# One-core streaming encoder layer: the out-projection's product halves one behind the other, its first token tile begun inside the last value product

## The chip, the cores and the metric

The kernel runs on one core of a Trainium2 chip. The metric is the device time of one execution in microseconds (us). Five engines run side by side, each working through its own instructions in a fixed order: PE multiplies matrices (PEld is its weight load), ACT and DVE do elementwise work, POOL does small elementwise work, SP issues the DMAs. The order on every engine is written when the kernel is built, by a planner that plays the program through with estimated durations and picks, for each engine, the ready instruction of the highest priority (roughly, the one written first). On the chip an instruction waits for semaphores but is never overtaken on its engine.

## What is computed

One inference step of a one-layer encoder, for 1024 prompt tokens and 32 tokens of a running stream (1056 in all), width 1024:

```
h  = mixer(rms_norm(x, g_mix_pre))          # proj = xn @ w_in, three kinds of recurrent heads
                                            # cat = heads' outputs, normed and gated
                                            # mixer returns cat @ w_out   <- the out-projection
x  = x + rms_norm(h, g_mix_post)
h  = conv_ffn(rms_norm(x, g_ffn_pre))       # up @ w_up, causal conv, gelu(gate)*val, @ w_down
x  = x + rms_norm(h, g_ffn_post)
```

All matrices are float32. A product is made of three passes of a faster format: an operand is split into a high part and a low part (high by a cast on ACT, low by a subtraction on DVE or POOL), and `mm3` adds high*high, high*low and low*high in PSUM. In the profile these are lines 100, 101 and 102.

## The kernel before

The tokens are nine tiles `u`: 0 to 7 of 128 prompt tokens, 8 of the 32 running tokens. Three groups `g` (tiles 0-2, 3-5, 6-8) pass through the input projection one after the other. In each, `inproj` makes the feature products, then the value and gate columns in blocks of 256 (`blk` 0 to 7; 0-3 values, 4-7 gates). For the last group `vg_across` makes them with the tokens across: for each of two halves `e` 24 matmuls (8 `k` times 3) into one PSUM bank `pv`, an ACT copy to an SBUF tile `vf` (line 460), and then, behind the next block's products, `back`: per token tile two PE transposes into a bank `pb` (line 448) and `vg_store`, which for the gates is tanh on ACT (line 420, recorded as line 112), one or two steps on DVE, a multiply on POOL (line 427) and a store to DRAM. `vf` is taken in the pool `p1` under the tag `x`.

The heads' recurrences, `mixer(u)`, are a side stream: a generator advanced a few steps after each step of the main stream (`merge`, `pump`). Its small matmuls (line 702) and DVE, ACT and POOL steps stand between the main stream's work on all engines. While the out-projection runs, the mixers of tiles 8, 6 and 7 are still going, in this order, each behind the one before; the out-projection's tiles come in the order `RING` = 0, 1, 2, 3, 8, 4, 5, and then 6 and 7.

The out-projection of a tile, `outproj(u)`, in parts divided by `yield`:

- load `cat` of the tile (`ct`, line 268) and the residual `xr` (line 275), and those of the next tile;
- for each half of the columns four transposes of `ct` into a bank `ctp` (line 1031), the split into `ch` (ACT, line 1035) and `cl` (DVE, line 1036), in the pool `p2`, three buffers each;
- the product `zp`: for each `k` of 8 the three matmuls of the first 512 columns and the three of the second, so that two PSUM banks fill side by side; for tile 0 `out_weights` splits the weight row `k` in front of it (`woh` by ACT, lines 106 and 1001; `wol` by DVE, lines 109 and 1003; from the raw rows `wor`);
- for each bank a square with its sum and a copy to `z` on ACT (lines 1066, 1067);
- the norm and the residual (POOL lines 1069, 218, 219; DVE lines 1076, 1077; ACT line 1081), and the transposes `fxt` of the result (PE line 1100, two banks; DVE line 1105), stored to DRAM for the FFN.

`pipeline` runs them so that a tile's transposes come before the last part of the tile two back, then the norm of the tile one back, then the tile's product. PSUM has one pool, `psb`, of three banks (tag `big`) for `pv`, `pb`, `ctp`, `zp` and `fxt`; the mixers have others, one of them the bank `mi` in two halves, handed out in turn by `small`.

SBUF is used again by pools that open and close: `p2`, with the 8-row tiles `woh` and `wol`, is opened where `p1` was closed. The FFN's first pools stand where the mixers' pools were.

Of the kernel before, what the change touches and what calls it, by code (L numbers as in the profile page):

```python
# [8 lines left out]
F32 = mybir.dt.float32  # L9
# [10 lines left out]
DEC = 32  # L20
# [70 lines left out]
def body(ctx: ExitStack, tc: tile.TileContext, a: dict):  # L91
# [163 lines left out]
    pws, wo_raw, ring = ExitStack(), [], []  # L255
    NRING, CT0 = 7, 6

    ct_of, xr_of, tail, xlate, mixed = {}, {}, [], {}, set()
# [11 lines left out]
    def load_res(u):  # L270
        if u in xr_of:
            return
        n = 128 if u < 8 else DEC
        xr_of[u] = (ring if u in RING else tail)[0](f"xr{u}")
        sp.dma_start(xr_of[u][:n], xsrc(128 * u, n))

    def units_of(g):
        t0, pl, sl = GROUPS[g]
        us = [(t0 // 128 + i, 128 * i, 128) for i in range(pl // 128)]
        if sl:  # L280
            us.append((8, pl, sl))
        return us
# [71 lines left out]
    def inproj(g, xh, xl, normed, scaled=None):  # L354
# [87 lines left out]
        def vg_across(blks):  # L442

            def back(blk, fs, part):
                for (u, off, n) in units_of(g)[part]:
                    ps = psb.tile([128, 256], F32, tag="big", name=f"pb{u}_{blk}")
                    for e in range(2):
                        pe.transpose(ps[:n, 128 * e:128 * e + 128], fs[e][:, off:off + n], ident)
                    vg_store(blk, u, off, n, ps)

            before = None
            for blk in blks:
                ws = vg_weights(blk)
                fs = p1.tile([128, 2, T], F32, tag="x", name=f"vf{blk}", bufs=3)
                fs = [fs[:, 0], fs[:, 1]]
                for e in range(2):
                    ps = psb.tile([128, T], F32, tag="big", name=f"pv{g}_{blk}_{e}")
                    for k in range(8):
                        mm3(ps, [w[:, 128 * e:128 * e + 128] for w in ws[k]], (xh[:, k, :], xl[:, k, :]), k == 0, k == 7)
                    act.copy(fs[e], ps)  # L460
# [207 lines left out]
        if g == 2:  # L668
            pfs.close()
            pw = pws.enter_context(tc.tile_pool(name="pw", bufs=1, side="left"))  # L670
            ring.append(lambda name: pw.tile([128, 1024], F32, tag="ring", name=name, bufs=NRING))
            for k in range(8):
                if k == CT0:
                    load_cat(0)
                wo_raw.append(ring[0](f"wor{k}"))
                sp.dma_start(wo_raw[k], a["w_out"][k])
# [327 lines left out]
            yield  # L1004


    def outproj(p2, W, u):

        gm, woh, wol = W[:3]
# [9 lines left out]
        ct = ct_of[u]  # L1019
        chs = []  # L1020
        for hf in range(2):
            if u < 7 or u == 8:
                ps = psb.tile([128, 4, 128], F32, tag="big", name=f"ctp{u}{hf}")
            else:
# [4 lines left out]
            for k in range(4):  # L1029
                c = 512 * hf + 128 * k  # L1030
                pe.transpose(ps[:, k, :n], ct[:n, c:c + 128], ident[:n, :n])
            ch = p2.tile([128, 4, 128], F32R, tag="ch", name=f"ch{u}{hf}", bufs=3)
            cl = p2.tile([128, 4, 128], F32R, tag="cl", name=f"cl{u}{hf}", bufs=3)
            with tc.high_priority(offset=AHEAD):
                ins = (act.copy(ch[:, :, :n], ps[:, :, :n]),
                       dve.tensor_tensor(cl[:, :, :n], ps[:, :, :n], ch[:, :, :n].bitcast(F32), op=ALU.subtract))
            if u == RING[0]:
                halves[:] = ins
            chs += [(ch[:, k, :n], cl[:, k, :n]) for k in range(4)]
        yield  # L1040
        ss = p2.tile([128, 4], F32, tag="oss", name=f"oss{u}", bufs=2)
        pss = [psb.tile([128, 512], F32, tag="big", name=f"zp{u}{hf}") if u != 7 else
               upper[0].tile([128, 512], F32, tag="xw", name=f"zp{u}{hf}", bufs=4) for hf in range(2)]
        cs = [slice(512 * hf, 512 * hf + 512) for hf in range(2)]
        if u == 7:

            jk = jks[0]
            for hf in range(2):
                for k in range(8):
                    mm3(pss[hf], chs[k], (woh[:, k, cs[hf]], wol[:, k, cs[hf]]), k == 0, k == 7)  # L1050
                with tc.high_priority(offset=AHEAD):
                    kept["jk"] = act.activation(jk, pss[hf], AF.Square, accum_out=ss[:, hf:hf + 1])
        else:
            for k in range(8):
                if u == RING[0]:
                    next(W[3])
                for hf in range(2):
                    mm3(pss[hf][:n], chs[k], (woh[:, k, cs[hf]], wol[:, k, cs[hf]]), k == 0, k == 7)
                if k == 3 and u == 6:
                    yield  # L1060
        load_res(u)
        x = xr_of[u]
        if u != 7:
            z = (ring if u in RING else tail)[0](f"z{u}")
            for hf in range(2):
                act.activation(z[:n, cs[hf]], pss[hf][:n], AF.Square, accum_out=ss[:n, hf:hf + 1])
                act.copy(z[:n, cs[hf]], pss[hf][:n])
# [44 lines left out]

    def pipeline(gens):

        for i in range(len(gens) + 2):
            for j in (i, i - 2, i - 1, i):
                if 0 <= j < len(gens) and i - 1 < len(gens):
                    next(gens[j])
                    yield


    def col_operands(pool_, q, s, between=lambda: None):
# [359 lines left out]
    pool.memset(x0[:, :, 1, smp:smp + 2], 0.0)  # L1482
    firsts = [outproj(p2, wo, u) for u in RING]
    merge(pipeline(firsts), 27, 3 * NMIX + 2)
    pump(1000)
    last = [outproj(p2, wo, u) for u in (6, 7)]
    for x in (last[0], last[0], last[1]):
        next(x)
    sp.dma_start(x0[:, :, 0, :], xn_d[:, :, 0:n0])
    sp.dma_start(x0[:, :, 1, :smp], xn_d[:, :, HW:HW + smp])  # L1490
    sp.dma_start(x0[:, :, 1, smp + 2:smp + 130], xn_d[:, :, fcol(4):fcol(5)])
# [210 lines left out]
```

## Time and profile before

| | |
|---|---|
| median of 3 runs | 1419.99 us (1419.96 to 1420.18) |
| the profiled execution: its time | 1421.18 us |
| the profiled execution: span from first to last instruction | 1419.4 us |
| PE busy | 1368.0 us (96%) |
| DVE busy | 1009.2 us (71%) |
| ACT busy | 711.3 us (50%) |
| POOL busy | 281.9 us (20%) |
| mean granted TensorE clock | 0.986 |

How to read the profile: times are microseconds from the span's start. A row of the timeline has start, duration, engine, line, operation, output and inputs, shapes and count; in brackets stands the idle time of the engine before it and what ended it. A row of the windows has the stretch, its length, then for PE, PEld, DVE, ACT and POOL the busy time and the number of instructions, then the TensorE clock that was granted (1.00 is full speed), the DMA share and GB/s. The matmuls' durations overlap their neighbours', so the pace of a row of matmuls is read from their starts.

### The profile page before, as it was taken

The page shows a single profiled execution, that of the slowest core. Times are in us where ns is not written, and L with a number is a line of the kernel's source. Part 1 is how long each engine was busy: PE and PEld are TensorE (multiplying, and loading weights), DVE is VectorE, ACT ScalarE, POOL GpSimd, SP SyncE. Part 2 cuts the span into 40 slices and gives each one's busy share as a digit, 9 for nine tenths or more (in the row PEclk, how much of TensorE's full clock was granted, in tenths as well). Part 3 has the DMA queues.
Part 4 walks back from the last instruction along what each step waited for, and adds up shares of the span by engine and source line. Part 5 has one row for each costly group of instructions (what it writes and reads, how often), then busy time and mean ns, then how long its engine had stood idle before and what let it go on. Part 6 is the DMA issues. An engine that isn't in the chain of part 4 may idle for free.

```text
span 1419.4 us, 30029 instructions
## 1 busy us (share of the span) xinstructions
PE 1368.0 (96%) x11804; PEld 1253.1 (88%) x11804; DVE 1009.2 (71%) x1818; ACT 711.3 (50%) x1403; POOL 281.9 (20%) x461
## 2 busy tenths in 40 slices
PE   6989999999999998899899999999999999999998
PEld 5989889998888876767799999999999999988886
DVE  4795469758687667676798887788888875654644
ACT  4555447445474545333755545554455544533432
POOL 5531211224112223212131111111111110000100
PEclk9999999999999989999999999999999999999999
DMA  9599779776789753344412221221222156765652
GB/s 344 191 338 342 242 238 309 232 254 210 270 281 341 256 179 125 129 145 102 138 50 99 79 91 70 91 76 73 79 82 85 62 199 239 235 221 169 245 176 100
DMA packets 132581, 255.11 MB, mean 180 GB/s; under 512 B 27639, under 2 KB 78487, under 8 KB 132439
## 3 DMA queue, kind: packets, MB, share of 16 engines
q1 hardware_dynamic: 132439, 253.19, 52.3%
q8 instruction: 92, 1.51, 0.4%
q14 instruction: 50, 0.41, 0.1%
HBM read 192.26 MB, written 60.89 MB: 178 GB/s over the span
## 4 chain that ended last, share of the span: by engine, by line
PE 78%; DVE 8%; DMA 5%; ACT 4%; issue 2%; POOL 2%; SPq 1%; DVEq 0%; POOLq 0%; ACTq 0%
PE pd L102 6%; PE pd L101 6%; PE pd L100 6%; PE pux L100 4%; PE pux L102 4%; PE pux L101 4%; PE pv L100 3%; PE pv L102 3%; PE pv L101 3%; PE puw L101 3%; PE puw L100 3%; PE puw L102 3%; PE zp L100 2%; PE pf L100 2%; PE pf L101 2%; PE zp L101 2%
## 5 line engine op out<-in xcount | busy, mean ns | idle before, releaser
L1276 DVE SCALAR_TENSOR_TENSOR y<-uu,fconv_sb,y 128x1060 f32<-128x1060 f32 x88 | 116.2, 1321 | 28.5 <-ACT y L1274 27.8
L102 PE MATMUL pd<-wd,hl 128*128 128x512 f32 x264 | 105.0, 399 | 0.0
L101 PE MATMUL pd<-wd,hh 128*128 128x512 f32 x264 | 104.1, 394 | 0.0
L100 PE MATMUL pd<-wd,hh 128*128 128x512 f32 x264 | 103.5, 393 | 0.0
L1270 POOL COPY uu<-uu 128x2 f32<-128x2 f32 x44 | 36.6, 831 | 214.2 <-DVE uu L1218 214.0
L1213 ACT COPY c<-pux 128x274 f32<-128x274 f32 (+1 forms) x132 | 49.3, 376 | 40.8 <-PE pux L102 39.5
L1274 ACT ACTIVATE y<-uu,fconv_sb 128x1060 f32<-128x1060 f32 x44 | 56.1, 1275 | 16.9 <-POOL uu L1271 15.6
L100 PE MATMUL zp<-woh,ch 128*128 128x512 f32 (+1 forms) x144 | 59.1, 414 | 5.3 <-DVE z L1105 5.2
L100 PE MATMUL pv<-wt_0h,xh 128*128 128x256 f32 (+2 forms) x195 | 58.6, 301 | 5.6 <-ACT xh L318 5.4
L101 PEld LDWEIGHTS pd<-wd,hh 128*128 128x128 f32 x264 | 49.6, 188 | 12.6
L100 PEld LDWEIGHTS pd<-wd,hh 128*128 128x128 f32 x264 | 49.6, 188 | 11.7
L102 PEld LDWEIGHTS pd<-wd,hl 128*128 128x128 f32 x264 | 49.6, 188 | 11.5
L101 PE MATMUL zp<-wol,ch 128*128 128x512 f32 (+1 forms) x144 | 58.4, 405 | 0.0
L102 PE MATMUL pv<-wt_0h,xl 128*128 128x256 f32 (+2 forms) x195 | 57.6, 296 | 0.4 <-DVE xl L319 0.4
L102 PE MATMUL zp<-woh,cl 128*128 128x512 f32 (+1 forms) x144 | 57.6, 403 | 0.0
L101 PE MATMUL pv<-wt_0l,xh 128*128 128x256 f32 (+2 forms) x195 | 57.2, 293 | 0.1
L100 PE MATMUL pv<-wt_1h,xh 128*128 128x256 f32 (+2 forms) x195 | 56.8, 291 | 0.0
L102 PE MATMUL pv<-wt_1h,xl 128*128 128x256 f32 (+2 forms) x195 | 56.7, 291 | 0.0
L101 PE MATMUL pv<-wt_1l,xh 128*128 128x256 f32 (+2 forms) x195 | 56.5, 290 | 0.0
L100 PE MATMUL pd<-hh,wd 128*128 128x288 f32 x176 | 52.0, 296 | 0.0
L101 PE MATMUL pd<-hl,wd 128*128 128x288 f32 x176 | 52.0, 296 | 0.0
L102 PE MATMUL pd<-hh,wd 128*128 128x288 f32 x176 | 51.8, 296 | 0.0
(1678 smaller groups left out, 5138.6 us busy)
## 6 DMA issues: line engine op xcount, KB each, us to landing
h_d<-y SPq DMA_DIRECT2D x22, 530.0 KB, 2.7
wt_0r<-in_w_tok SPq DMA_DIRECT2D x21, 512.0 KB, 6.1
wt_1r<-in_w_tok SPq DMA_DIRECT2D x21, 512.0 KB, 6.5
wt_0l<-lt_d SPq DMA_DIRECT2D x14, 512.0 KB, 7.1
wt_1l<-lt_d SPq DMA_DIRECT2D x14, 512.0 KB, 7.6
hr<-h_d SPq DMA_DIRECT2D x44, 128.0 KB, 3.1
hr<-h_d SPq DMA_DIRECT2D x22, 192.0 KB, 3.2
x<-in_xp SPq DMA_DIRECT2D x8, 512.0 KB, 7.6
```

Source lines behind the costliest of these rows:

```text
L100: pe.matmul(ps, lh[0], rh[0], start=first, stop=False, **kw)
L101: pe.matmul(ps, lh[0], rh[1], start=False, stop=False, **kw)
L102: return pe.matmul(ps, lh[1], rh[0], start=False, stop=last, **kw)
L1213: kept[name] = act.copy(t, ps)
L1270: pool.tensor_copy(u[:, GAP_P:GAP_P + 2], u[:, GAP_S - 2:GAP_S])
L1274: act.activation(y, u, AF.Identity, scale=fconv[:, j, 2:3], bias=fconv[:, j, 3:4])
L1276: dve.scalar_tensor_tensor(y, uu[i][:, s:s + NCOL], fconv[:, j, s:s + 1], y, op0=ALU.mult, op1=ALU.add)
```

## The change

It does four things. The tile `vf` gets a pool of its own, `pvf`, opened when group 2's feature pools close and closed after tile 0's product. In the last block of `vg_across` the transposes back of the block before all go behind `k` = 3 of the first half, and behind `k` = 3 of the second half stand the first four transposes and the split of the out-projection's tile 0 (`cat_half`, into `pvf`); the last block's own are written behind its second half, tiles 6 and 7 in one bank (`both`), and tile 8 of the last two blocks in a half of the bank `mi`. The product of every tile of `RING` but the first is made one half of the columns behind the other, each followed by its square and copy, and `pipeline` puts the next tile's transposes behind the halves: first half, the next tile's first four transposes, second half, the next tile's other four, the last part of the tile before, the norm of this one. The residual `xr` is loaded after the transposes, for the own tile alone, no longer one tile ahead; the FFN's first columns `xg0` are opened, and the two gap columns cleared, after tile 0's product.

```diff
@@ vg_across (inproj)
             def back(blk, fs, part):
+                late = blk >= blks[-1] - 1
+                both = psb.tile([128, 2, 256], F32, tag="big", name=f"pb67_{blk}") if blk == blks[-1] else None
                 for (u, off, n) in units_of(g)[part]:
-                    ps = psb.tile([128, 256], F32, tag="big", name=f"pb{u}_{blk}")
+                    ps = small(256) if late and u == 8 else both[:, u - 6] if both is not None else \
+                        psb.tile([128, 256], F32, tag="big", name=f"pb{u}_{blk}")
...
-                fs = p1.tile([128, 2, T], F32, tag="x", name=f"vf{blk}", bufs=3)
+                fs = vfs[0].tile([128, 2, T], F32, tag="vf", name=f"vf{blk}", bufs=3)
                 fs = [fs[:, 0], fs[:, 1]]
+                last = blk == blks[-1]
                 for e in range(2):
                     ps = psb.tile([128, T], F32, tag="big", name=f"pv{g}_{blk}_{e}")
                     for k in range(8):
                         mm3(ps, [w[:, 128 * e:128 * e + 128] for w in ws[k]], (xh[:, k, :], xl[:, k, :]), k == 0, k == 7)
+                        if last and k == 3:
+                            if not e:
+                                back(*before, slice(0, 3))
+                            else:
+                                first_half.append(cat_half(vfs[0], RING[0], 0))
                     act.copy(fs[e], ps)
-                    if before:
+                    if before and not last:
                         back(*before, slice(e, 1 + 2 * e))
                     yield
                 before = (blk, fs)
                 yield
-            for e in range(2):
-                back(*before, slice(e, 1 + 2 * e))
+            back(*before, slice(0, 3))
@@ inproj, g == 2, behind pfs.close() and the ring's pool
+            vfs.append(pvs.enter_context(tc.tile_pool(name="pvf", bufs=1, side="left")))
@@ outproj
+    def cat_half(p, u, hf, ps=None, **kw):
+        n = 128 if u < 8 else DEC
+        if ps is None:
+            ps = psb.tile([128, 4, 128], F32, tag="big", name=f"ctp{u}{hf}")
+        for k in range(4):
+            c = 512 * hf + 128 * k
+            pe.transpose(ps[:, k, :n], ct_of[u][:n, c:c + 128], ident[:n, :n])
+        ch = p.tile([128, 4, 128], F32R, tag="ch", name=f"ch{u}{hf}", **kw)
+        cl = p.tile([128, 4, 128], F32R, tag="cl", name=f"cl{u}{hf}", **kw)
...
+        return [(ch[:, k, :n], cl[:, k, :n]) for k in range(4)]
...
         load_cat(u)
         if u in RING:
-            load_res(u)
-            nxt = (RING + (6,))[RING.index(u) + 1]
-            load_cat(nxt)
-            if nxt in RING:
-                load_res(nxt)
+            load_cat((RING + (6,))[RING.index(u) + 1])
...
+            chs += first_half.pop() if u == RING[0] and not hf else cat_half(p2, u, hf, ps, bufs=3)
+            if u in RING:
+                yield
+        if u not in RING:
+            yield
+        if u in RING:
+            load_res(u)
...
+        def leave(ps, hf):
+            act.activation(z[:n, cs[hf]], ps[:n], AF.Square, accum_out=ss[:n, hf:hf + 1])
+            act.copy(z[:n, cs[hf]], ps[:n])
+
+        if u == RING[0]:
+            pss = [bank(hf) for hf in range(2)]
+            for k in range(8):
+                next(W[3])
+                for hf in range(2):
+                    product(pss[hf], hf, k)
+            z = ring[0](f"z{u}")
+            for hf in range(2):
+                leave(pss[hf], hf)
+            first_columns()
+            yield
+        elif u in RING:
+            z = ring[0](f"z{u}")
+            for hf in range(2):
+                ps = bank(hf)
+                for k in range(8):
+                    product(ps, hf, k)
+                leave(ps, hf)
+                if not hf:
+                    yield
...
     def pipeline(gens):
-        for i in range(len(gens) + 2):
-            for j in (i, i - 2, i - 1, i):
-                if 0 <= j < len(gens) and i - 1 < len(gens):
-                    next(gens[j])
-                    yield
+        next(gens[0])
+        next(gens[0])
+        yield
+        for i, x in enumerate(gens):
+            after = gens[i + 1:i + 2]
+            next(x)
+            yield
+            for y in after:
+                next(y)
+            yield
+            next(x)
+            yield
+            for y in after + gens[i - 1:i] + [x]:
+                next(y)
+            yield
...
-    x0 = p3s.enter_context(tc.tile_pool(name="p3", bufs=1, side="right")).tile([128, 8, 2, SUBS[0][1]], F32, name="xg0")
-    xlate[0] = x0
-    pool.memset(x0[:, :, 1, smp:smp + 2], 0.0)
+    def first_columns():
+        pvs.close()
+        xlate[0] = p3s.enter_context(tc.tile_pool(name="p3", bufs=1, side="right")).tile(
+            [128, 8, 2, SUBS[0][1]], F32, name="xg0")
+        pool.memset(xlate[0][:, :, 1, smp:smp + 2], 0.0)
...
-    merge(pipeline(firsts), 27, 3 * NMIX + 2)
+    merge(pipeline(firsts), 26, 3 * NMIX + 2)
```

Tiles 6 and 7 keep the order of their products as it was.

More of the change, by code (lines that the diff above doesn't have):

```diff
@@ L1028, in outproj @@
                 ps = both[:, hf]
[L1029 to L1036, printed above, removed]
@@ new lines, in outproj @@
+        if u == RING[0]:
+            pss = [bank(hf) for hf in range(2)]
[17 more added lines that the diff above has]
+                    yield
+        elif u == 6:
+            pss = [bank(hf) for hf in range(2)]
+            for k in range(8):
+                for hf in range(2):
+                    product(pss[hf], hf, k)
+                if k == 3:
+                    yield
+            z = tail[0](f"z{u}")
+            for hf in range(2):
+                leave(pss[hf], hf)
+        else:
+            pss = [bank(hf) for hf in range(2)]
@@ L1049, in outproj @@
                 for k in range(8):
-                    mm3(pss[hf], chs[k], (woh[:, k, cs[hf]], wol[:, k, cs[hf]]), k == 0, k == 7)
+                    product(pss[hf], hf, k)
                 with tc.high_priority(offset=AHEAD):
                     kept["jk"] = act.activation(jk, pss[hf], AF.Square, accum_out=ss[:, hf:hf + 1])
[L1053 to L1060, printed above, removed]
         load_res(u)
         x = xr_of[u]
[L1063 to L1067, printed above, removed]
         yield
```

27 lines of the change are left out of this document (15 added, 12 removed).

## The prediction

> **What bounds the kernel now.** I read the page first: busy times and the chain that ended last.
>
> ```profile
> PE 1368.0 (96%) x11804; PEld 1253.1 (88%) x11804; DVE 1009.2 (71%) x1818; ACT 711.3 (50%) x1403; POOL 281.9 (20%) x461
> PE 78%; DVE 8%; DMA 5%; ACT 4%; issue 2%; POOL 2%; SPq 1%; DVEq 0%; POOLq 0%; ACTq 0%
> ```
>
> PE is the bound of the whole, so a gain must be PE's idle time or PE's slow time. The change touches one stage, from the end of the last value product to the end of tile 7's product, so I asked for the windows of that stage, cut where the granted clock changes.
>
> ```profile
> core 0: us, PE busy (x) PEld busy (x) DVE busy (x) ACT busy (x) POOL busy (x), PEclk, DMA share, GB/s
> 511.10:515.40 4.30, 3.89 (x84) 2.71 (x83) 3.15 (x11) 1.10 (x4) 1.46 (x3) 0.99 0.09 30
> 515.40:529.00 13.60, 12.80 (x59) 9.05 (x58) 10.75 (x22) 9.71 (x13) 3.19 (x4) 0.50 0.90 301
> 529.00:538.70 9.70, 9.70 (x55) 7.59 (x54) 3.06 (x4) 1.66 (x5) 0.00 (x0) 1.00 0.64 202
> 538.70:604.00 65.30, 56.54 (x637) 45.29 (x637) 52.42 (x112) 30.71 (x77) 24.17 (x33) 1.00 0.37 121
> 604.00:607.50 3.50, 3.50 (x20) 2.08 (x15) 3.50 (x9) 0.72 (x2) 0.00 (x0) 0.51 0.00 0
> 607.50:664.00 56.50, 53.85 (x600) 39.88 (x597) 36.38 (x83) 19.13 (x45) 12.72 (x25) 1.00 0.39 118
> 664.00:689.30 25.30, 25.30 (x122) 20.86 (x122) 21.59 (x26) 16.43 (x33) 4.29 (x8) 1.00 0.59 187
> ```
>
> Two things are to be seen. From 515.4 to 529.0 PE ran at half clock: 12.80 us of work that would take 6.4 at full clock. And from 538.7 to 664 PE stood idle for 8.76 + 2.65 = 11.4 us. Third, PE's waits in that last stretch, to see what the idle time was for (waited for; total, times, longest), the largest of them:
>
> ```profile
> PE zp L100 <- DVE z L1105: 5.2, 3, 2.9
> PE om L702 <- DVE w L927: 2.3, 1, 2.3
> PE ctp L1031 <- ACT z L1067: 1.4, 1, 1.4
> PE fxt L1100 <- DVE z L1105: 0.6, 1, 0.6
> PE fxt L1100 <- ACT z L1067: 0.6, 1, 0.6
> ```
>
> Four of these are not waits for data. The product `zp`, the transposes `ctp` and `fxt` wait until ACT or DVE has read an older bank out: there are three banks, and the product holds two. They make 5.2 + 1.4 + 0.6 + 0.6 = 7.8 us. Only the 2.3 is a mixer's. Fourth, the timelines around tile 0:
>
> ```profile
> 510.76 0.30 PE L102 MATMUL pv<-xh,wt_1l 128*128 128x288 f32 x1
> 510.90 0.60 PE L448 MATMUL pb<-ident,vf 128*128 128x128 f32 x4
> 511.10 0.40 ACT L460 COPY vf<-pv 128x288 f32<-128x288 f32 x1 [2.73 <-PE pv L102]
> 515.36 1.99 ACT L106 CAST woh<-wor 128x1024 fp32r<-128x1024 f32 x2 [1.54 <-PE pb L448]
> 520.27 1.12 PE L1031 MATMUL ctp<-ident,ct 128*128 128x128 f32 x4 [0.61 <-ACT vth L112]
> 521.04 0.78 PE L100 MATMUL zp<-woh,ch 128*128 128x512 f32 x1
> 526.88 4.82 DVE L1003 TENSOR_TENSOR wol<-wor,woh 128x1024 fp32r<-128x1024 f32 x4
> 538.35 0.39 PE L102 MATMUL zp<-woh,cl 128*128 128x512 f32 x1
> ```
>
> The last value product ends at 511.06, but tile 0's begins at 521.04 and ends at 538.7. ACT's first weight cast waited for the transposes `pb`: `woh` lies where `p1` was, and `p1` held `vf`, which those transposes read last. And `ctp` waited 0.61 us for a bank that a tanh still had to read.
>
> **The change part by part.** First, the start of tile 0. With `vf` in its own pool the first cast waits for the last value product and ACT's copy behind it, so it starts at 511.5 instead of 515.36, 3.9 us earlier.
>
> ```profile
> L106 ACT CAST woh<-wor x2: 1040/1042/1044, 515.4 to 516.3; 128x1024 fp32r<-128x1024 f32 x2
> L109 DVE TENSOR_TENSOR wol<-wor,woh x2: 1218/1222/1225, 516.4 to 517.6; 128x1024 fp32r<-128x1024 f32 x2
> 549.08 0.39 PE L102 MATMUL zp<-woh,cl 128*128 128x512 f32 x1
> 551.80 0.39 PE L102 MATMUL zp<-woh,cl 128*128 128x512 f32 x1
> ```
>
> One cast and one subtraction later, at 511.5 + 1.04 + 1.22 = 513.8, the first product can run, since its `ch` and `cl` (first half) are ready by then. How early can tile 0 end? By DVE: its last weight subtraction ended at 531.70; 3.9 earlier is 527.8. The rows of 549.08 and 551.80 are twelve matmuls apart, 0.227 us each; six follow the last subtraction, so 529.2. By PE: 27.6 us from 511.1 to 538.7, less 1.2 idle, less 6.4 for the half clock, leaves 20.0 us of work, so 531.1: 7.6 us earlier if the clock doesn't fall. If it falls as before at 515.4, it should return as long after the first dense product as now (529.0 - 521.04 = 8.0), at 521.8. Then 6.4 us at half clock cost 3.2, the end is 534.3, and the gain 4.4. I take 5, near the second, because what stands before 515.4 stays transposes and small mixer matmuls. The moved transposes themselves cost nothing new: the block's own six and tile 0's eight were there before, four in 0.60 us or less; inside the value product they wait for nothing, since tile 0's `cat` is loaded long before.
>
> The banks `both` and `mi`: tiles 6 and 7 in one bank leave one for `ctp`, which takes the 0.61 (inside the 5). In exchange tile 7's transposes may wait for tile 6's tanh, and a mixer's matmul for tile 8's: 0 to 0.61 each, two blocks, at most 1.2. PE has value products or tile 0's to run beside it, so I take 0 and keep 1.2.
>
> Second, the products one half behind the other, six tiles.
>
> ```profile
> L1066 ACT ACTIVATE z<-zp x16: 581/598/651, 538.3 to 684.1; 128x512 f32<-128x512 f32 x14, 32x512 f32<-32x512 f32 x2
> L1067 ACT COPY z<-zp x16: 557/585/661, 539.9 to 687.2; 128x512 f32<-128x512 f32 x14, 32x512 f32<-32x512 f32 x2
> ```
>
> The matmuls are the same 48 a tile. A half is 24 x 0.227 = 5.4 us, and its bank is read out in 0.60 + 0.59 = 1.2. So the first half leaves under the second, and behind a product PE waits for one bank where it waited for two. I take half of the 7.8 away: 4. The ends are all of it, 7.8, and below nothing: another wait of 0.6 for each of five later tiles, 3 us lost. The ACT work is the same; where it stands in ACT's queue is the second rival.
>
> Third, the queues. On SP the load of `xr` comes one tile later.
>
> ```profile
> DMA to landing us min/median/max: 2.6/4.7/7.5
> 515.38 0.11 POOL L1482 MEMSET xg<- 128x16 f32 x1 [0.16 <-PE pb L448]
> ```
>
> It lands in 4.7 us, 7.5 at most, and its reader, DVE's add, comes behind the own product of 10.9 us: hidden; without that cover it would cost up to 7.5 per tile. The loads of `cat` keep their lead of one tile. POOL's 0.11 us for the gap columns move behind tile 0; the pool's first other user is the FFN. The 26 for 27 in `merge` moves the mixers' steps by a twenty-seventh. All this I count at nothing.
>
> What is late next: tile 7 and the FFN's beginning.
>
> ```profile
> 665.42 0.87 POOL L906 TENSOR_TENSOR cat<-cat,gt 128x320 f32<-128x320 f32 x1
> 666.32 0.33 SPq L1160 DMA_DIRECT2D wu0r<-in_w_up  x1
> 678.28 0.48 PE L100 MATMUL zp<-woh,ch 128*128 128x512 f32 x1
> ```
>
> Mixer 7 delivers the last part of its `cat` at 666.29, and tile 7's product begins at 678.28. Transposes (0.60), cast and subtraction (an estimate: half of the weights' 1.04 and 1.22, as half as wide) lie between, so 10 us are slack: a gain of 9 on PE fits even if the mixers stood still. But the FFN's first load leaves right behind mixer 7, so the mixers must move too.
>
> The sum: 5 + 4 = 9 us off the span of 1419.4, 1410.4. The profiled execution took 1421.18, 1.8 more than its span and 1.2 more than the median; so 1412.2 for a profiled one, and 1411.0 beside the median of 1419.99.
>
> **The rivals.** First, the mixers set the end. Mixers 8, 6 and 7 follow one another, and DVE is busy 52.42 of 65.3 us. If mixer 7 still ends at 666.3, the FFN starts as before, and only DVE's idle time from 664.0 to 689.3 can be gained, 25.3 - 21.59 = 3.7. I would expect 1.5 of it, 1418.5. Against it speaks who waits for whom between 510 and 680:
>
> ```profile
> DVE cl L1036 <- ACT ch L1035: 11.6, 5, 6.6
> DVE S L872 <- PE mi L702: 6.6, 4, 4.4
> DVE hn L965 <- PE om L702: 3.4, 1, 3.4
> ACT z L1066 <- PE zp L102: 41.3, 6, 13.9
> ```
>
> The mixers' DVE steps wait 6.6 + 3.4 for PE, PE only 2.3 for theirs. They are pushed back by the products and should move up with them.
>
> Second, slower: ACT held. ACT takes its queue in order; six times it stood at the head of a tile's square, 41.3 us in all, and in these six holds DVE waited 11.6 us for casts behind it, 1.9 a hold. With two squares per tile there are six holds more, now with mixers' exponentials behind them. At 1.9 each that is 11.6 us and takes the 4 away too: -5 + 11.6 = 6.6 slower, 1426.6. It decides from 1.5 us a hold (9 / 6). Against it: the first half's square waits while the second half's matmuls run, so PE has work.
>
> Third, the clock stays down as long. If the half clock lasts its 13.6 us wherever the products begin, of the first term only the 1.2 us of idle time are left, and 1.2 + 4 = 5.2 give 1414.8. For it: the long stretch held 12.80 us of instructions and still did not raise the clock until eight us of dense products; against it: those began late. [...]
>
> **How the numbers follow.** A measurement here can tell about 0.2%, 2.8 us, from no change. Forecast 0.50, mixers 0.17, ACT held 0.17, clock 0.16. The forecast and the clock rival lie beyond 2.8 us on the fast side (0.49 and 0.16), of the mixers' rival 0.05 does: faster 0.70. Its other 0.12 and 0.01 of the forecast are the same: 0.13. Slower 0.17. The forecast's own ends: 7.6 + 7.8 off, and 1.8 more if the half clock at 604 goes, 17.2, 1402.8; and 4.4 - 3 - 1.2 off, about nothing. The range from 1403 to 1422 holds these and the mixers' rival, and cuts off most of the held ACT (0.12) and a little at the fast end (0.04).
>
> **What would show it.** Right: the first `woh` cast at about 511.5 behind the copy `vf` and not behind `pb`; tile 0's last `zp` between 531 and 535; less than 8 us at half clock around it; the bank waits of `zp`, `ctp` and `fxt` at about 4 us in sum; mixer 7's last `cat` and the load `wu0r` about 9 us earlier; from there on the FFN's length unchanged. Wrong: `cat` of tile 7 still at 666 (first rival); ACT's waits for `zp` longer in sum and DVE or PE waiting behind ACT (second); 13 us at half clock (third). New waits of PE inside the last value product would break the first term.

## The result, and the profile after

The changed kernel takes 1428.04 us (median of six runs, 1426.94 to 1429.13); the kernel before, on the same chip and in the same set, 1421.59. The ratio is 1.0044, with a 95% interval from 1.003 to 1.0059: slower by 6 us. The forecast was 1411.0, faster. The profiled execution took 1426.94 us with a span of 1425.2, 5.8 more than before.

From the head of the kernel after's page, its span and the engines' busy times:

```profile
span 1425.2 us, 30044 instructions
...
PE 1368.0 (96%) x11804; PEld 1253.2 (88%) x11804; DVE 1008.2 (71%) x1818; ACT 711.1 (50%) x1403; POOL 279.0 (20%) x461
```

PE is busy for the same 1368.0 us as before. What was lost is idle time of PE: 57.2 us against 51.4. The windows of the stage, with the same bounds as in the prediction, show that it didn't come where the change begins:

```profile
511.10:515.40 4.30, 3.54 (x29) 2.33 (x26) 3.95 (x6) 4.30 (x6) 0.77 (x2) 1.00 0.79 240
515.40:529.00 13.60, 12.53 (x72) 9.65 (x72) 9.93 (x20) 8.39 (x17) 3.76 (x6) 1.00 0.61 194
529.00:538.70 9.70, 9.70 (x53) 7.77 (x52) 5.16 (x7) 4.44 (x11) 0.75 (x2) 1.00 0.81 292
538.70:604.00 65.30, 55.80 (x612) 42.74 (x610) 45.55 (x99) 25.23 (x61) 20.85 (x28) 0.90 0.36 117
604.00:607.50 3.50, 3.50 (x19) 1.93 (x18) 3.44 (x10) 1.62 (x4) 2.08 (x2) 1.00 0.43 108
607.50:664.00 56.50, 55.31 (x620) 43.05 (x620) 36.59 (x85) 17.85 (x43) 13.74 (x23) 0.91 0.33 106
```

The granted clock (the last column but two) is 1.00 up to 538.7: the half clock of 13.6 us before is gone. Behind 538.7 it is 0.90 and 0.91, where before it was 1.00 but for 3.5 us. Now the timeline of tile 0 and of its surroundings:

```profile
510.91 2.00 ACT L106 CAST woh<-wor 128x1024 fp32r<-128x1024 f32 x2
512.01 0.50 PE L100 MATMUL zp<-woh,ch 128*128 128x512 f32 x1
526.02 0.39 PE L102 MATMUL zp<-woh,cl 128*128 128x512 f32 x1
```

Tile 0's product starts 9.0 us earlier than before and ends at 526.4, 12.3 us earlier. PE's waits from 510 to 695 follow (total, times, longest):

```profile
PE ctp L1027 <- DMA ct<-cat_d: 4.6, 1, 4.6
PE zp L100 <- DVE cl L1032: 2.5, 1, 2.5
PE sc L713 <- DVE P L807: 2.3, 2, 1.9
...
PE fxt L1151 <- DVE cl L1032: 0.8, 1, 0.8
...
PE zp L100 <- ACT z L1074: 0.3, 1, 0.3
```

Of the 7.8 us of waits for banks, 3.6 are left: the 0.3, and also the 2.5 and the 0.8, since the matmuls of line 100 read `ch` and the transposes `fxt` read `z`; neither reads `cl`, so they waited for the bank `ctp` that the subtraction still had to read. Both intended effects are there, then, and still the kernel is slower. Where they went is seen at the mixers. First the last steps of mixer 7, the FFN's first load, and the first and last matmul of tile 7's product:

```profile
674.36 0.88 POOL L917 TENSOR_TENSOR cat<-cat,gt 128x320 f32<-128x320 f32 x1 [0.60 <-DVE cat L915]
675.27 0.33 SPq L1222 DMA_DIRECT2D wu0r<-in_w_up  x1
682.42 0.48 PE L100 MATMUL zp<-woh,ch 128*128 128x512 f32 x1
693.18 0.39 PE L102 MATMUL zp<-woh,cl 128*128 128x512 f32 x1
```

Mixer 7 delivers its last `cat` at 675.24, 8.95 us later than before (666.29), and tile 7's product starts 4.14 us later (before 678.28). So the delay is not in the products but in the mixers, and it can be followed back to the first of them. The groups of instructions that write or read the bank `mi` between 498 and 535, first before, then after (the two times are the first and last start):

```profile
L702 PE MATMUL mi<-ident,kh x4: 272/272/273, 502.4 to 507.2; 128*32 128x128 f32 x4
```

```profile
L452 PE MATMUL mi<-ident,vf x4: 270/272/285, 500.1 to 511.5; 128*32 128x128 f32 x4
L112 ACT ACTIVATE vth<-mi x2: 375/375/375, 509.4 to 524.8; 32x256 f32<-32x256 f32 x2
L713 PE MATMUL mi<-ident,kh x4: 271/272/272, 526.2 to 530.8; 128*32 128x128 f32 x4
```

`mi<-ident,kh` is mixer 8's transposition of its decayed keys, without which its state can't be updated. Before, it ran at 502.4 to 507.2, inside the value products. After, tile 8's gate transposes (`mi<-ident,vf`) take the halves of `mi` from 500.1 and 511.3 on, the tanh that frees the second half runs only at 524.8, and the keys follow at 526.2: 24 us late. ACT's timeline shows what stands in front of that tanh; a row of DVE and one of POOL follow:

```profile
512.80 0.39 ACT L112 ACTIVATE vth<-pb 128x256 f32<-128x256 f32 x1
513.08 0.59 ACT L1031 CAST ch<-ctp 128x512 fp32r<-128x512 f32 x1
513.55 4.86 ACT L1012 CAST woh<-wor 128x1024 fp32r<-128x1024 f32 x5
518.28 0.40 ACT L112 ACTIVATE vth<-pb 128x256 f32<-128x256 f32 x1
...
524.80 0.38 ACT L112 ACTIVATE vth<-mi 32x256 f32<-32x256 f32 x1 [2.81 <-POOL vg L427]
```

```profile
522.43 0.29 DVE L425 TENSOR_SCALAR vth<-vth 128x256 f32<-128x256 f32 x1
522.80 1.97 POOL L427 TENSOR_TENSOR vg<-vth,gh 128x256 f32<-128x256 f32 x1 [2.09 <-DVE vth L425]
```

The tanhs of tiles 6 and 7 and the earlier weight casts come first on ACT. But tile 7's tanh is done at 518.68, and tile 8's starts 6.1 us later: there is one buffer `vth` (`bufs=1` in the kernel), so tile 8's tanh can't write before POOL's multiply for tile 7 has read it, to 524.77. That multiply waited for DVE's step at 522.43, which stands behind weight subtractions. For the last 2.81 us ACT stood at the tanh and waited. No view of PE's waits names this: PE's wait for `mi` is 0.5 us in all, because the order on PE puts the keys behind the tanh from the start.

### The profile page after: what moved, and what is told of

Its sections match the earlier page's. It is cut to its first block, busy times and chain, and to the rows that moved or that the text cites. A ratio compares the mean times of both kernels' runs of the same rounds, so it can differ in the third digit from the quotient of the medians.

```text
span 1425.2 us, 30044 instructions
## 1 busy us (share of the span) xinstructions
PE 1368.0 (96%) x11804; PEld 1253.2 (88%) x11804; DVE 1008.2 (71%) x1818; ACT 711.1 (50%) x1403; POOL 279.0 (20%) x461
## 4 chain that ended last, share of the span: by engine, by line
PE 59%; DVE 2%; ACT 1%; POOL 1%; DMA 1%; issue 1%; DVEq 0%; POOLq 0%; ACTq 0%
PE pd L102 6%; PE pd L101 6%; PE pd L100 6%; PE pux L102 4%; PE pux L100 4%; PE pux L101 4%; PE puw L100 3%; PE puw L101 3%; PE puw L102 3%; PE zp L100 2%; PE zp L101 2%; PE zp L102 2%; PE puy L102 1%; PE puz L100 1%; PE puy L100 1%; PE puy L101 1%
## 5 line engine op out<-in xcount | busy, mean ns | idle before, releaser
L1332 POOL COPY uu<-uu 128x2 f32<-128x2 f32 x44 | 31.9, 724 | 205.9 <-DVE uu L1280 205.8
L1336 ACT ACTIVATE y<-uu,fconv_sb 128x1060 f32<-128x1060 f32 x44 | 56.1, 1274 | 23.8 <-POOL uu L1333 23.1
L100 PEld LDWEIGHTS pd<-wd,hh 128*128 128x128 f32 x264 | 49.6, 188 | 11.6
```

The source lines that it names most:

```text
L100: pe.matmul(ps, lh[0], rh[0], start=first, stop=False, **kw)
L1332: pool.tensor_copy(u[:, GAP_P:GAP_P + 2], u[:, GAP_S - 2:GAP_S])
L1336: act.activation(y, u, AF.Identity, scale=fconv[:, j, 2:3], bias=fconv[:, j, 3:4])
```

## The experiments

Four theories. **A**: the half of `mi` that tile 8 holds until its tanh keeps mixer 8 back, the mixers' chain (8, 6, 7) carries the delay to its end, and this sets when tile 7 and the FFN can start. **B**: the earlier weights and tile 0 displace mixer 8 on DVE and ACT. **C**: the product halves and the new order of the steps let the products run ahead, up to tile 8, whose `cat` isn't there yet. **The forecast's reading**: PE's queue sets the end. Each ratio is to runs of the kernel before in the same set. The four columns behind it come from one profiled execution of each kernel; in "early start alone", "halves alone" and "after, tile 8 first" that was the slowest of its set, in the kernel after, "after, `mi` in the last block alone" and "after, shared bank in both blocks" the fastest.

| kernel | ratio to before (95%) | mixer 8's first key transpose, us | mixer 7's last `cat` ends, us | tile 7's last matmul ends, us | span |
|---|---|---|---|---|---|
| before | 1 | 502.4 | 666.3 | 689.4 | 1419.4 |
| after | 1.0044 (1.0030 to 1.0059) | 526.2 | 675.2 | 693.6 | 1425.2 |
| after, tile 8 in the big pool | 0.9947 (0.9925 to 0.9970) | 500.6 | 658.0 | 680.6 | 1412.3 |
| early start alone | 0.9996 (0.9979 to 1.0012) | 530.1 | 674.5 | 693.9 | 1423.8 |
| halves alone | 0.9956 (0.9943 to 0.9969) | 503.6 | 661.9 | 684.5 | 1416.3 |
| after, tile 8 sixth | 1.0050 (1.0029 to 1.0071) | 529.0 | 675.1 | 696.8 | 1426.2 |
| before, tile 8 in `mi` | 1.0047 (1.0034 to 1.0060) | 529.1 | 678.3 | 696.7 | 1427.9 |
| early start, tile 8 in the big pool | 0.9970 (0.9952 to 0.9987) | 502.2 | 662.8 | 687.7 | 1419.0 |
| before, fewer product matmuls | 0.9980 (0.9965 to 0.9994) | 501.8 | 671.3 | 689.5 | 1420.5 |
| mixers six steps ahead | 0.9970 (0.9948 to 0.9992) | 499.8 | 660.7 | 686.2 | 1416.6 |
| mixers first on all engines | 0.9994 (0.9980 to 1.0009) | 497.3 | 653.3 | 688.8 | 1417.6 |
| before, one mixer level fewer | 0.9972 (0.9959 to 0.9984) | 500.0 | 648.8 | 685.0 | 1413.3 |
| after, `mi` in the last block alone | 1.0048 (1.0031 to 1.0064) | 528.7 | 672.9 | 693.8 | 1423.6 |
| after, shared bank in both blocks | 0.9947 (0.9932 to 0.9961) | 501.4 | 656.5 | 679.0 | 1410.6 |
| after, tile 8 first | 0.9945 (0.9928 to 0.9963) | 516.1 | 664.2 | 683.9 | 1414.5 |

Two things hold in all fifteen. From the end of tile 7's product to the end of the span it is always 728.3 to 731.8 us, so that product's end decides the time to some 3.5 us. And it ends at least 18.2 us behind mixer 7's `cat`: 18.3 in the kernel after, 18.4 in "before, tile 8 in `mi`", 23.1 before, 36 where the mixers are far ahead. I read it so that the end is the later of two: `cat` plus 18.3 us, or PE's queue.

**Tile 8 back in the big pool.** On the kernel after:

```
-  ps = small(256) if late and u == 8 else both[:, u - 6] if both is not None else \
+  ps = both[:, u - 6] if both is not None and u < 8 else \
       psb.tile([128, 256], F32, tag="big", name=f"pb{u}_{blk}")
```

> Tile 8's last two value transposes go into a bank of the big PSUM pool instead of a half of the small bank mi; all else as in the kernel after. Theory A (the half of mi that tile 8 holds until its tanh at 524.8 us keeps mixer 8's key transposes and state update back by 13 us, and the mixers' chain sets when the FFN's first load can go): the transposes of kh of mixer 8 stand near 502-508 us again (526.3 and 530.7 in the kernel after), the FFN's first load leaves 5 to 9 us earlier than 675.3, and the time is 1418 to 1422 us. Theory B (the earlier weights' split and first tile displace mixer 8 on VectorE and ScalarE) and theory C (product halves and the new order of the tiles' steps let the products run ahead of the mixers): the transposes stay above 515 us or the gain is lost by 600 us, and the time stays at 1426 to 1428 us.

Measured: 0.9947, median 1413.99 us. Its `mi` group and the last step of its mixer 7:

```profile
L713 PE MATMUL mi<-ident,kh x4: 271/272/272, 500.6 to 504.3; 128*32 128x128 f32 x4
```

```profile
657.13 0.89 POOL L917 TENSOR_TENSOR cat<-cat,gt 128x320 f32<-128x320 f32 x1 [1.92 <-DVE cat L915]
```

The keys are back at 500.6, the `cat` 17.2 us earlier than in the kernel after. One line turns a loss of 0.44% into a gain of 0.53%, more than theory A promised (1418 to 1422); C is out as the main cause. B is not, for the line moves tile 0 too:

| kernel | last value product ends, us | tile 0's product starts, us | ends, us | PE busy with mixer matmuls between the first and the last of these, us |
|---|---|---|---|---|
| before | 511.06 | 521.04 | 538.74 | 8.46 |
| after | 510.58 | 512.01 | 526.41 | 0.71 |
| after, tile 8 in the big pool | 510.59 | 519.71 | 534.90 | 7.48 |
| early start, tile 8 in the big pool | 512.18 | 521.31 | 537.30 | 8.76 |
| after, tile 8 first | 512.95 | 517.63 | 531.07 | 1.85 |

With tile 8 back in the big pool, the mixers' matmuls stand before and inside tile 0's product again, as before the change, and most of the early start is gone (9.1 us behind the last value product instead of 1.4). So the early start of the kernel after and its late mixer 8 come together, and this pair alone doesn't say which causes the other.

**Each half of the change alone.** The early start with the old products, the old `pipeline` and the old loads of `xr` (the product's part of the edit):

```
+  pss = [bank(hf) for hf in range(2)]
+  for k in range(8):
+      for hf in range(2):
+          product(pss[hf], hf, k)
...
-      ps = bank(hf)
-      for k in range(8):
-          product(ps, hf, k)
-      leave(ps, hf)
-      if not hf:
-          yield
+      leave(pss[hf], hf)
...
```

> The early start alone: value tiles in their own pool, last value block's order and banks, first half of tile 0's transposes early, as in the kernel after; but both product halves together, the old order of the tiles' steps, and residual rows loaded as in the kernel before. Theory A and theory B: mixer 8 is late here too, its last cat at or after 575 us, the FFN's first load at 672 us or later, time 1425 to 1431 us. Theory C: the mixers are not behind, tile 8's transposes do not wait for cat, the first load is at 657 to 666 us and the time 1411 to 1420 us.

Measured 0.9996, no difference, with a median of 1422.57 us below theory A's range; in the profiled execution the keys stand at 530.1 and the first load at 674.6, as A and B had it and C had not, but that is the slowest of ten that spread widely (1417.70 to 1425.58 us). Why the hold doesn't make this kernel slower than the one before stays open. The halves and the new `pipeline` on the kernel before, `vf` and the last block unchanged:

> The product halves one behind the other and the new order of the tiles' steps alone, on the kernel before: value tiles, last value block and the start of tile 0 as before. Theory C: mixers 6 and 7 fall behind, the FFN's first load is at 670 us or later, time 1424 to 1429 us. Theories A and B: mixer 8 keeps its times (kt at 502 to 514 us), the bank waits of 7.8 us go, and the time is 1414 to 1420 us; 1419 to 1420 if the mixers alone set the end.

Measured 0.9956: theories A and B again, C is refuted. The halves alone are a gain of 0.44%.

**Tile 8 later in the order.** On the kernel after:

```
-  RING = (0, 1, 2, 3, 8, 4, 5)
+  RING = (0, 1, 2, 3, 4, 8, 5)
```

> The kernel after with tile 8 sixth instead of fifth in the order of the tiles (0, 1, 2, 3, 4, 8, 5). The wait of tile 8's transposes for its cat (4.63 us, and 10 us of half clock about it) should be gone. If that stall sets the end (part of theory C): time lower by 4 to 9 us, 1418 to 1423 us. If the mixers' chain sets the end and the products only wait on its account (theory A or B): mixer 8's last cat stays at 576 us, the first load stays at 673 to 676 us, and the time is 1425 to 1428 us.

Measured 1.0050. The wait of 4.63 us is gone from PE's list, and the time and mixer 7's `cat` (675.1) are the same: that wait was not what set the end.

**The hold put into the kernel before, and taken out of the early start.** The second puts the line of the first experiment (tile 8 back in the big pool) on the early start alone. The first is this edit on the kernel before:

```
-  ps = psb.tile([128, 256], F32, tag="big", name=f"pb{u}_{blk}")
+  ps = small(256) if u == 8 and blk >= blks[-1] - 1 else \
+      psb.tile([128, 256], F32, tag="big", name=f"pb{u}_{blk}")
```

> The kernel before with one thing of the change: tile 8's value transposes of the last two blocks go into a half of the bank mi instead of a bank of the big pool. Theory A (a half of mi held until the tanh keeps mixer 8's key transposes and update back, and the last mixer's cat sets the FFN's start): mixer 8's transposes of kh move from 502-507 us to 525 us or later, the FFN's first load leaves at 671 us or later instead of 666.3, and the time is 5 to 12 us above before. Rivals B and C (the early work, or the halves and the order): within 2 us of before.

> The early start without the hold: the kernel with the early start alone (old products and old order of steps), and tile 8's transposes in the big pool. Theory A: the 9 to 10 us that the first load moved in the same pair with the new products come here too, first load at 662 to 666 us, time 1412 to 1417 us. Theory B (early work displaces mixer 8): first load stays at 672 us or later, time 1421 to 1425 us.

Measured 1.0047 and 0.9970. Of the first, the `mi` groups and mixer 7's last step:

```profile
L112 ACT ACTIVATE vth<-mi x2: 373/373/373, 512.1 to 527.6; 32x256 f32<-32x256 f32 x2
L703 PE MATMUL mi<-ident,kh x4: 272/272/273, 529.1 to 531.0; 128*32 128x128 f32 x4
```

```profile
677.41 0.88 POOL L907 TENSOR_TENSOR cat<-cat,gt 128x320 f32<-128x320 f32 x1 [0.61 <-DVE cat L905]
```

The one expression alone makes the kernel before as slow as the whole change does. Without it the early start gains 0.30%, a little less than expected (median 1418.08 us). The price of the hold is not one number: 0.47% on the kernel before, 0.26% on the early start alone (its two intervals overlap), 0.97% on the kernel after. Theory A is borne out from both sides, but B is not out yet: the run without the hold has no early tile 0 (the table above), and in the kernel before with `mi` it moved forward, from 10.0 to 6.3 us behind the last value product. The last experiment below separates them.

**What sets the end: work taken from each chain.** From the products, on the kernel before, the low half of the weights left out for tiles 1 to 3:

```
+  if u in (1, 2, 3):
+      pe.matmul(pss[hf][:n], chs[k][0], woh[:, k, cs[hf]], start=k == 0, stop=False)
+      pe.matmul(pss[hf][:n], chs[k][1], woh[:, k, cs[hf]], start=False, stop=k == 7)
+      continue
```

> The kernel before with the second of the three matmuls of each product step (the low half of the weights) left out for tiles 1, 2 and 3: 3 x 16 matmuls of 0.389 us, 18.7 us less work on PE, between 540 and 640 us; nothing of the mixers is touched. My forecast's reading (PE's queue sets the end, and the mixers move up with the products): first load and end 10 to 18 us earlier, time 1402 to 1411 us. Rival 1 of the forecast (the mixers' own chain on VectorE, ScalarE and GpSimd sets the FFN's start): mixer 7's last cat stays at 663 to 666 us, and the time is 1418 to 1421 us.

From the mixers, one level of the decay tree left out of 6 and 7:

```
-  levels = [c for c in LEVELS if 2 * c <= cl]
+  levels = [c for c in LEVELS if 2 * c <= cl and not (c == 4 and u in (6, 7))]
```

> The kernel before with one of the six levels of the decay tree (blocks of 4) left out of mixers 6 and 7: some 4 us of each mixer's chain by the spacing of the levels' stores into P, nearly no work on PE beside the 18.7 us that were taken from the products in the run before. If the mixers' chain sets the FFN's start: first load 5 to 9 us earlier than 666.3, time 1411 to 1416 us. If PE's queue sets it: first load within 2 us, time 1418 to 1421 us.

In the first the time fell by 0.2%, not by the 10 to 18 us of the forecast's reading. But the run relieved PE less than its expectation says. The 18.7 us add up durations of 0.389 us that overlap; by their starts, 0.227 us apart, the 48 matmuls are 10.9 us at full clock. And the granted clock was 0.90 from 538.7 to 604 and 0.94 from there to 664 (before 1.00 and 0.97), so that PE's busy time in the whole fell from 1368.0 to 1363.7 us, by 4.3. Nor did `cat` stay: it came 5.0 us later, and tile 7's product ended 18.2 us behind it, at the mixers' bound. So this run doesn't show what a relieved PE would give. Why its mixers came later, though nothing of theirs was touched, stays open: clock and planned order both changed, and no run separates them.

With one level less in two mixers the first load left 17.3 us earlier, more than expected, and the time fell by 0.28% (median 1417.03 us, between the ranges of the two branches); there the product ended 36.2 us behind `cat`, so the mixers no longer set the end, and I take it that PE's queue did. Before, the two chains are 4.8 us apart (23.1 less 18.3): a gain of the mixers was worth little, and a delay beyond that counts.

**The mixers put ahead**, both on the kernel with tile 8 in the big pool: six steps earlier among the projections, or all their instructions ahead of the products' copies.

```
-  n_side = (0, 3 * NMIX - 6, 3 * NMIX)[g]
+  n_side = (0, 3 * NMIX - 6, 3 * NMIX + 6)[g]
```

```
-  next(side[0])
+  with tc.high_priority(offset=AHEAD) if ahead[0] else ExitStack():
+      next(side[0])
...
+  ahead[0] = True
```

> The kernel after with tile 8's transposes in the big pool, and the mixers' steps taken 6 steps earlier among the last group's projections (57 instead of 51 steps there). If the mixers' chain sets the FFN's start: mixer 7's last cat 3 to 10 us earlier than in the kernel with the transposes alone moved (657.1 us), time 1404 to 1411 us. If PE's whole work sets it: the steps only change places, cat within 2 us, time 1412 to 1416 us. If the last group's projections have no room on VectorE or PE for them, tile 0 starts later and the time is 1416 us or more.

> The kernel after with tile 8's transposes in the big pool, and every instruction of the mixers (not TensorE's alone) ranked ahead of the products' copies and norms from the first tile on. If the mixers' chain sets the FFN's start and waits in queues behind the products' copies: mixer 7's last cat 4 to 10 us earlier than 657.1, time 1404 to 1410 us. If the chain is bound by its own steps: cat within 2 us of 657.1, time 1412 to 1416 us. If the products then come late and set the end instead: tile 7's product after 685 us, time 1416 us or more.

Measured 0.9970 and 0.9994, both no better than without (0.9947). In the second `cat` comes 4.8 us earlier, and tile 7's product 8.3 us later: the third case of its expectation. The first moved tile 0's start to 524.9 us, and its `cat` comes 2.6 us later than without. In the one that did favour the mixers, the products paid.

**How long `mi` is held.** `mi` in the last block alone, and a version for the big pool's banks (tiles 6 and 7 in one bank in both late blocks, tile 8 in the big pool):

```
-  late = blk >= blks[-1] - 1
+  late = blk == blks[-1]
```

> The kernel after with only the last block's tile 8 transposes in mi; those of the block before it go to the big pool. Theory A with the hold up to 509 us as its cause: mixer 8's key transposes back at 500-508 us, first load at 657 to 663 us, time 1411 to 1416 us. Theory A with the hold from 511 to 525 us as its cause: key transposes still behind the last tanh, first load at 672 us or later, time 1424 to 1428 us.

> The kernel after with no transposes in mi, and tiles 6 and 7 sharing one bank of the big pool in both of the last two blocks instead of the last alone, so that tile 0's banks come free sooner: its first product at 514 to 518 us instead of 519.7. If the mixers' chain sets the FFN's start: first load within 2 us of 658.9, time 1412 to 1416 us. If tile 0's start counts too: first load 2 to 5 us earlier, time 1408 to 1412 us.

The first is as slow as the change (1.0048; tanh at 527.2, keys at 528.7): the second hold alone does it. The second gives 0.9947, the same as with three banks; tile 0 started no sooner (520.3 against 519.7). Last, `mi` kept in both blocks and only given back sooner:

```
-  for (u, off, n) in units_of(g)[part]:
+  for (u, off, n) in sorted(units_of(g)[part], key=lambda t: late and t[0] < 8):
```

> The kernel after with one change of order: in the last two blocks tile 8's transposes and tanh come before those of tiles 6 and 7 instead of behind them; they still lie in mi, and no bank is added. If the length of the hold (511.3 to 524.8 us, until ScalarE reaches the tanh behind tiles 6 and 7 and the weight casts) delays mixer 8: its key transposes stand at 510 to 518 us instead of 526 and 531, the first load leaves at 657 to 668 us, time 1411 to 1420 us. If it is mi's use as such that costs (the alternating halves, the order planned around it): key transposes and first load as in the kernel after (526 us, 675 us), time 1425 to 1428 us.

Measured 0.9945, median 1414.09 us. Its groups on `mi` and the keys on PE's timeline:

```profile
L452 PE MATMUL mi<-ident,vf x4: 270/271/272, 503.2 to 514.3; 128*32 128x128 f32 x4
L112 ACT ACTIVATE vth<-mi x2: 368/370/372, 508.8 to 515.7; 32x256 f32<-32x256 f32 x2
```

```profile
516.08 0.39 PE L713 MATMUL mi<-ident,kh 128*32 128x128 f32 x2 [1.00 <-ACT vth L112]
```

The tanh ends at 516.1 instead of 525.2, the keys follow at once, and here the profile does name the wait. In the six kernels that hold tile 8 in `mi` the keys stand 0.4 to 2.7 us behind the start of the last tanh, wherever that lies. And here tile 0 is early: its product ends 18.1 us behind the last value product (27.7 before, 15.8 in the kernel after), with 1.85 us of mixer matmuls in between, and still mixer 8 isn't late and the kernel gains. That puts B out as the main cause: it is the length of the hold, not the use of `mi` and not the early tile 0. The windows of the same kernel:

```profile
538.70:604.00 65.30, 65.13 (x664) 48.20 (x664) 53.06 (x119) 30.41 (x76) 19.56 (x31) 1.00 0.51 159
```

PE is now busy for all but 0.17 of 65.3 us, at full clock; the kernel after stood idle there for 9.5.

Three versions beat the kernel before by the same amount, 0.53 to 0.55%: tile 8 in the big pool, the same with the shared bank twice, and tile 8 first. Their intervals overlap, with that of the halves alone (0.44%) too, so the runs don't rank them, and that the early start adds anything to the halves is not shown.

## Why the prediction was wrong

**Wrong: the step "The banks `both` and `mi`".** It said that "a mixer's matmul for tile 8's" may wait "0 to 0.61 each, two blocks, at most 1.2. PE has value products or tile 0's to run beside it, so I take 0 and keep 1.2". The bound came from the one wait of a transpose for a tanh in the trace before, 0.61 us. But how long the half is held is not that row: it is the time from tile 8's transposes to its tanh, 13.5 us here, behind the tanhs of two other tiles and the one buffer `vth`, and so behind the weight casts on ACT and the weight subtractions on DVE which the same change moved up. And that PE has other work is no cover, since it is not PE that is late but the mixer; its keys came 23.8 us later. The prediction read who waits for whom in the trace before, but didn't ask which of mixer 8's steps need `mi`. The hold alone costs 0.47% on the kernel before, and turns the rest of the change from 0.9947 to 1.0044.

**Wrong by size: the slack of 10 us** between mixer 7's `cat` and tile 7's product. It counted bare durations between them: 0.60 + 0.52 + 0.61, or 1.7 us of the 12.0. In the kernel after they are 7.2 us apart (675.24 to 682.42): the last transposes run at 678.79, the cast at 679.90 and the subtraction at 680.72, behind the FFN's first casts. From `cat` to the product's end it was 18.2 to 18.4 us in the three kernels where it was shortest, so I take 7.2 as the least; the slack was then 4.8 and not 10. The 8.95 us by which `cat` came later, less 4.8, are the 4.15 by which the product did. The span grew by 1.7 more behind that product; this I have not followed.

**Term 1: the start right, its worth not shown.** The first cast went at 510.91 (forecast 511.5) behind the copy `vf`, and the clock didn't fall around tile 0. By the prediction's sum that alone ends the tile at 531.1; it ended at 526.4. The rest is no gain: the mixer matmuls, 8.46 us of PE in this stretch before, were down to 0.71 and came later. What the early start is worth, the runs leave open. In the run without the hold that gained 0.30%, tile 0's product starts at 521.31, no earlier than before; with an early tile 0 and the hold (early start alone) the time is unchanged; and tile 8 first, with an early tile 0, is no faster than tile 8 in the big pool, nearly without. The forecast's 5 us are neither confirmed nor refuted.

**Right: term 2.** The bank waits went from 7.8 to 3.6 us (forecast about 4); the halves alone gave 0.44%, 6.3 us (forecast 4). Without the hold the whole change gains 0.53%, some 7.5 us (4 to 11 by its interval), where the sum had 9; the runs can't tell these apart.

**Rivals.** The first, that the mixers set the end, had the right chain but took them to stand still at 666.3; they moved back. What a mixer later than 666 would cost was worked out nowhere, and the forecast's counter-argument (the mixers "should move up with them") failed, because the bank of one of their steps was tied to a tanh. The second, ACT held at the squares, didn't happen:

```profile
ACT z L1073 <- PE zp L102: 23.2, 8, 8.5
```

It was 41.3 us before, in six waits instead of eight, and DVE's wait for the casts `ch` went from 11.6 to 10.3. This rival had the right sign and nearly the right time (1426.6) for a wrong reason: luck. The third, the clock, didn't happen either: 1.00 throughout tile 0. That it fell later, to 0.90 and 0.91, the prediction didn't forecast; the version with tile 8 first also shows 0.91 behind 604 and is fast. The moved transposes took 0.60 us per four (at 508.92, between value products), with a granted clock of 1.00 from 507 to 511; what transposes by themselves do to the clock is not shown.

The queues (`xr` one tile later, the memset, the 26 for 27) show no wait of their own in PE's list. On POOL the memset stood 5.2 us at the head, to 520.60, and waited for a matmul of tile 0's product; POOL's next step, at 522.80, waited for DVE anyway.

## What to carry to other kernels

Before a step borrows a buffer from another stream, look up who else uses it and when it is given back: the price is the time until its last reader runs, on that reader's queue as the change leaves it and behind what that reader needs in turn (here one buffer that three engines pass on), and it is paid by the other stream, not by the engine that stays busy. Where two chains meet at one point, work out the slack between them first, with the queues in it and not the bare durations: a gain on the later chain counts until the other becomes the later one, and a delay on the earlier chain costs what exceeds the slack. An edit of one line can change the planned order elsewhere: look up in the trace whether what it was to test, here the early tile 0, is still there. A hold planned into the order need not show in a list of waits (in the kernel after PE's wait for `mi` was 0.5 us in all, and the keys came 23.8 us later): compare when the same instructions start in both traces.

## What the runs showed of the hardware

Half clock came inside a gap of PE of 1.92 us. The timeline of the kernel after about that gap, then windows of one microsecond (clock in the last column but two):

```profile
575.66 0.69 PE L713 MATMUL sc<-Qz,Ld 64*64 64x64 f32 x32
578.27 1.13 PE L713 MATMUL sc<-Qz,Ld 64*64 64x64 f32 x32 [1.92 <-DVE P L807]
584.02 0.63 PE L1027 MATMUL ctp<-ident,ct 32*128 32x32 f32 x4 [4.63 <-DMA ct<-cat_d]
```

```profile
576.00:577.00 1.00, 0.35 (x25) 0.21 (x16) 0.78 (x3) 0.97 (x3) 0.41 (x2) 1.00 0.06 16
577.00:578.00 1.00, 0.00 (x0) 0.00 (x0) 1.00 (x2) 0.07 (x1) 0.63 (x1) 0.61 0.00 0
587.00:588.00 1.00, 1.00 (x5) 0.81 (x4) 0.00 (x0) 0.00 (x0) 0.00 (x0) 0.77 0.00 0
```

PE is idle from 576.35 to 578.27, and the mean clock of 0.61 from 577 to 578, with 1.00 before and 0.50 behind it, puts the fall at about 577.2, 0.9 us into the gap. Ahead of it stood small matmuls of a mixer (the row of 575.66); what part they had in the fall, this trace doesn't separate. It rose again inside the microsecond from 587, at about 587.5, 3.5 us after PE had dense work from 584.02 (0.98 to 1.00 us busy in each microsecond).
